# Output projection of the attention heads: seven products for eight in six of eight column pairs

## The chip, the cores and the metric

One Trainium2 chip, of which the program uses one core. The metric is the time of one execution on the device in microseconds (us). A core has five engines that run beside each other and each take their instructions in order: PE (TensorE, matrix products), DVE (VectorE), ACT (ScalarE), POOL (GpSimd) and SP (SyncE, which here only issues DMAs). DMAs move data between DRAM and the on-chip memory; matrix products write to PSUM banks, from which DVE or ACT fetch the result. "Evacuating" a bank means that fetch.

## The reference

One encoder layer over two requests of 256 tokens (512 columns here), model width 2048:

```python
xn = rmsnorm(h, norm_mix_w)
proj = xn @ w_in
y_na = neighbourhood_attention(na(0), na(1), na(2), na_rpb)      # 8 heads of 128
y_dn = gated_deltanet_bidir(...)                                  # 8 heads of 128
mixed = jnp.concatenate([y_na, y_dn.astype(h.dtype)], axis=-1) @ w_out
h = h + mixed
hn = rmsnorm(h, norm_ffn_w)
return h + (jax.nn.silu(hn @ w_gate) * (hn @ w_up)) @ w_down
```

The change concerns `mixed`, and of it the half that multiplies the attention heads `y_na` with the upper half of `w_out`. That is a product of a 2048 x 1024 matrix (transposed weights) with 1024 x 512.

## The kernel before

All activations lie transposed: features on the 128 partitions, the 512 token columns along the free side; the first 256 columns are one request, the last 256 the other. Products are made as exactly as float32 needs: each operand is split into a rounded part (`hi`) and the rest (`lo`), and `mm3` issues three matrix products for one, hi x hi, hi x lo and lo x hi. The split of a weight tile is one ACT instruction (`hi`, line 138) and one DVE subtraction (`lo`, line 139). The helper `half_gemm` makes a 128 x 512 result from a 128 x 1024 weight tile with eight times `mm3`, 24 matrix products of 512 columns:

```python
def load_w(src, shape):                                                     # 143
    raw = wp.tile([P] + shape, F32, tag="raw", bufs=3, name="w_raw")
    nc.sync.dma_start(raw, src)
    hi = wp.tile([P] + shape, F32R, tag="hi", bufs=3, name="w_hi")
    lo = wp.tile([P] + shape, F32R, tag="lo", bufs=3, name="w_lo")
    with tc.high_priority(offset=AHEAD):
        split(hi, lo, raw)
```

Each of the tags `raw`, `hi` and `lo` has three buffers, and so has the PSUM tag `g` of the pool `pg`, in which the results arise. So the fourth tile after one waits until that one's buffer is free: a weight split waits for the products of three tiles earlier, and a product waits until the result of three products earlier is evacuated. Tiles keep their engine's program order, which the scheduler fixes when the program is built; `tc.high_priority` moves instructions ahead in it. PE's order is that of the code.

Small work of other stages is spread between the products: `pump()` advances generators by one step (`chains`, `side`). While the attention half of the output projection runs, the last two heads of the recurrence (`recur`, heads 6 and 7) finish this way, and after them `finish_pair`: squares of the outputs on ACT (line 876), a reciprocal root by Newton steps on DVE (lines 880 to 882), a scaling on DVE (line 887), and after a pause of five pumps eight transposes on PE (line 90) with what follows (lines 903, 141, 142).

The stage itself, lines 950 to 972: the attention heads are read back from DRAM (`s_na`) into `nml`, split into `nmh` and `nml`, and the residual input `xT` is read into `h1`. Then, over the sixteen column tiles `i` in the order 0, 8, 1, 9, ..., one `half_gemm` each, the result is added to `h1` on DVE (line 969) and stored to DRAM as `s_h1` by a DMA on POOL (line 971):

```python
for i in pairs:                                                             # 965
    ps = pg.tile([P, T], F32, tag="g", name="ps_g")
    half_gemm(ps, w_out[i, 0], nas, True, True)
    hk = h1[i // 8][:, i % 8]
    tt(hk, hk, ps, ALU.add)
    if i not in pairs[:2]:
        nc.gpsimd.dma_start(s_h1[i], hk)
```

The next stage, lines 973 to 1031, does the other half (`half_gemm` with `dns`, the recurrence's heads), reads `s_h1` into `hk` (SP, line 1006), adds the product on DVE (line 1009), stores `s_h2` on POOL (line 1010) and prepares the operands of the feed-forward stage. That stage uses a seven-products scheme of its own (`block`), which the change does not alter.

## Time and profile before

| | |
|---|---|
| times of three runs | 2252.09, 2252.39, 2252.64 us; median 2252.39 |
| the profiled execution | 2253.6 us, of which the span from first to last instruction is 2251.8 us |
| clock of TensorE granted in it | 0.998 |
| the stage that the change rewrites | about 742 to 842 us of the span |
| the stage after it, also touched | about 842 to 932 us |
| stores of `s_h1` late in the first of them | every 5.44 us, one per `half_gemm` |

A row of the profile names line, engine, operation, `out<-in` and the shape; "x" is a count, "busy" a sum in us, "mean" in ns, and after the second bar stands the engine's idle time just before these instructions with what ended it. Matrix products overlap in the records, so the pace is read from their starts, not from their durations. A DMA row of a queue ends with the KB of one and the median us from issue to landing.

### The profile page before, as it was taken

The page shows a single profiled execution, that of the slowest core. Times are in us where ns is not written, and L with a number is a line of the kernel's source. Part 1 is how long each engine was busy: PE and PEld are TensorE (multiplying, and loading weights), DVE is VectorE, ACT ScalarE, POOL GpSimd, SP SyncE. Part 2 cuts the span into 40 slices and gives each one's busy share as a digit, 9 for nine tenths or more (in the row PEclk, how much of TensorE's full clock was granted, in tenths as well). Part 3 has the DMA queues.
Part 4 walks back from the last instruction along what each step waited for, and adds up shares of the span by engine and source line. Part 5 has one row for each costly group of instructions (what it writes and reads, how often), then busy time and mean ns, then how long its engine had stood idle before and what let it go on. Part 6 is the DMA issues. An engine that isn't in the chain of part 4 may idle for free.

```text
span 2251.8 us, 32459 instructions
## 1 busy us (share of the span) xinstructions
PE 2238.1 (99%) x12308; PEld 1918.6 (85%) x12308; DVE 1776.8 (79%) x2726; ACT 1031.3 (46%) x1550; POOL 236.6 (11%) x370
## 2 busy tenths in 40 slices
PE   9999999999999999999999999999999999999998
PEld 7888888888888888888888888888888888888888
DVE  7954799974555637888888888888888798898966
ACT  6664433333434325544444444444444464444435
POOL 1321000010000010101101111101100001001010
PEclk9999999999999999999999999999999999999999
DMA  5344322354333555677777777777777467667682
GB/s 210 130 141 144 111 97 95 100 145 133 103 104 103 195 175 190 208 205 205 200 208 200 200 192 203 216 203 204 200 197 194 147 179 210 176 179 205 176 205 86
DMA packets 112540, 381.20 MB, mean 169 GB/s; under 512 B 14048, under 2 KB 14640, under 8 KB 112128
## 3 DMA queue, kind: packets, MB, share of 16 engines
q1 hardware_dynamic: 77552, 266.25, 35.3%
q0 software_dynamic: 33680, 110.78, 23.7%
q8 instruction: 97, 1.59, 0.3%
q10 hardware_dynamic: 1152, 2.10, 0.3%
q14 instruction: 59, 0.48, 0.1%
HBM read 343.66 MB, written 35.41 MB: 168 GB/s over the span
## 4 chain that ended last, share of the span: by engine, by line
PE 91%; DVE 4%; DMA 2%; issue 1%; ACT 1%; POOL 0%; SPq 0%; DVEq 0%; ACTq 0%; POOLq 0%
PE ps_g L87 32%; PE ps_c L87 14%; PE ps_d L87 14%; PE ps_a L87 14%; PE ps_b L87 7%; PE ps_s L87 7%; DMA w_raw<-in_w_in_dram 1%; DVE w_lo L139 1%; DVE prod L587 1%; DVE W L589 1%; PE ps_o L87 1%; DMA kkq<-s_gram 1%; PE ps_s L90 1%; PE ps_e L87 0%; ACT w_hi L138 0%
## 5 line engine op out<-in xcount | busy, mean ns | idle before, releaser
L87 PE MATMUL ps_g<-xhi,w_hi 128*128 128x512 f32 x880 | 351.6, 400 | 0.0
L87 PE MATMUL ps_g<-xhi,w_lo 128*128 128x512 f32 x880 | 343.4, 390 | 0.8 <-DVE w_lo L139 0.8
L87 PE MATMUL ps_g<-xlo,w_hi 128*128 128x512 f32 x880 | 343.2, 390 | 0.6 <-DVE xlo L257 0.6
L138 ACT ACTIVATE w_hi<-w_raw 128x1024 fp32r<-128x1024 f32 x164 | 173.3, 1058 | 275.7 <-PE ps_g L87 209.6
L138 ACT ACTIVATE w_hi<-b 128x1024 fp32r<-128x1024 f32 (+1 forms) x180 | 185.8, 1032 | 237.8 <-issue 119.2
L139 DVE TENSOR_TENSOR w_lo<-w_raw,w_hi 128x1024 fp32r<-128x1024 f32 x164 | 200.4, 1222 | 111.1 <-ACT w_hi L138 110.9
L138 ACT ACTIVATE w_hi<-w_first 128x1024 fp32r<-128x1024 f32 (+1 forms) x180 | 185.4, 1030 | 180.9 <-PE ps_c L87 90.8
L139 DVE TENSOR_TENSOR w_lo<-w_first,w_hi 128x1024 fp32r<-128x1024 f32 (+1 forms) x180 | 213.8, 1188 | 60.2 <-ACT w_hi L138 56.7
L139 DVE TENSOR_TENSOR w_lo<-b,w_hi 128x1024 fp32r<-128x1024 f32 (+1 forms) x180 | 213.1, 1184 | 7.2 <-ACT w_hi L138 6.7
L87 PEld LDWEIGHTS ps_g<-xhi,w_lo 128*128 128x128 f32 x880 | 165.2, 188 | 36.8 <-DVE w_lo L139 1.3
L87 PEld LDWEIGHTS ps_g<-xhi,w_hi 128*128 128x128 f32 x880 | 165.4, 188 | 36.3 <-issue 2.9
L87 PEld LDWEIGHTS ps_g<-xlo,w_hi 128*128 128x128 f32 x880 | 165.4, 188 | 33.9 <-DVE xlo L257 1.6
L87 PE MATMUL ps_d<-xc,w_hi 128*128 128x512 f32 x704 | 175.1, 391 | 0.0
L87 PE MATMUL ps_c<-xc,w_hi 128*128 128x512 f32 x704 | 175.1, 391 | 0.0
L87 PE MATMUL ps_a<-xc,w_hi 128*128 128x512 f32 x696 | 173.1, 391 | 0.0
L87 PEld LDWEIGHTS ps_c<-xc,w_hi 128*128 128x128 f32 x704 | 129.4, 188 | 25.0
L87 PEld LDWEIGHTS ps_d<-xc,w_hi 128*128 128x128 f32 x704 | 129.3, 188 | 25.0
L87 PEld LDWEIGHTS ps_a<-xc,w_hi 128*128 128x128 f32 x696 | 127.9, 188 | 24.8
L138 ACT ACTIVATE w_hi<-w_second 128x1024 fp32r<-128x1024 f32 (+1 forms) x60 | 62.0, 1033 | 93.2 <-DVE ga L1153 50.3
L87 PE MATMUL ps_d<-xc,w_lo 128*128 128x256 f32 x704 | 98.5, 283 | 0.0
L87 PE MATMUL ps_c<-xc,w_lo 128*128 128x256 f32 x704 | 98.5, 283 | 0.0
L87 PE MATMUL ps_a<-xc,w_lo 128*128 128x256 f32 x696 | 97.4, 283 | 0.0
(390 smaller groups left out, 4209.6 us busy)
## 6 DMA issues: line engine op xcount, KB each, us to landing
w_raw<-in_w_in_dram SPq DMA_DIRECT2D x108, 512.0 KB, 3.3
b<-in_w_gate_dram SPq DMA_DIRECT2D x66, 512.0 KB, 4.1
b<-in_w_up_dram SPq DMA_DIRECT2D x66, 512.0 KB, 4.9
b<-in_w_group_dram SPq DMA_DIRECT2D x48, 448.0 KB, 4.3
w_raw<-in_w_out_dram SPq DMA_DIRECT2D x32, 512.0 KB, 3.6
w_raw<-in_w_down_dram SPq DMA_DIRECT2D x24, 512.0 KB, 3.7
w_second<-in_w_gate_dram SPq DMA_DIRECT2D x22, 512.0 KB, 7.3
w_first<-in_w_gate_dram SPq DMA_DIRECT2D x22, 512.0 KB, 4.5
```

Source lines behind the costliest of these rows:

```text
L87: pin(nc.tensor.matmul(*a, **k))
L90: pin(nc.tensor.transpose(*a))
L138: act(out=hi, in_=src, func=AF.Copy)
L139: tt(lo, src, r32(hi), ALU.subtract)
L587: stt(pv, W[:, s0:s1, s0:c], ndm[:, c:c + 1], kkq[:, c, 0, None, s0:c].broadcast_to([P, n, j]), ALU.mult, ALU.mult)
L589: nc.vector.tensor_reduce(W[:, s0:s1, c], pv, AX.X, ALU.add)
```

## The change

Column tiles are taken in pairs (j, j + 8). The first two pairs (`MIX_PLAIN = 2`) are computed as before, with the result copied out by ACT and stored without the residual. Each of the other six pairs becomes a `mix_block`: the pair's two output tiles, the two halves of the attention heads (0 to 3 and 4 to 7) and the two requests form a 2 x 2 product of blocks, and a scheme with seven products and sums of blocks is used in place of eight. Each of the seven multiplies a 128 x 512 weight tile (four heads) with 256 columns: 4 times `mm3`, 12 matrix products of 256 columns. Below they are called p0 to p6 in their order; their weights are b11, b21, `second`, `first` and its two further sums, with b22 before the last (p0 b11, p1 b21, p2 `second`, p3 `first`, p4 `first` + b22, p5 b22, p6 that sum + b21).

- Sums of token blocks (`token_sums`, once, 12 instructions on POOL, 16 for the splits) are made while the plain pairs run, from a second read of `s_na` into `nsum`.
- Sums of weight blocks: two on DVE (lines 1023, 1024), two on POOL (lines 1048, 1053). The `lo` of p5's weights (line 956) is made on POOL in place of DVE. Three sums of results are on POOL (lines 1050, 1054, 1055).
- The residual `xT` is no longer added here. The next stage reads `s_h1` on SP (line 1072) and adds `xT` by an accumulating DMA on POOL (line 964), and its buffer `hk` has three copies in place of two.

```diff
+MIX_PLAIN = 2
...
+    def w_split(src, minus=tt):
+        n = src.shape[1]
+        hi = wp.tile([P, 8, P], F32R, tag="hi", bufs=3, name="w_hi")[:, :n]
+        lo = wp.tile([P, 8, P], F32R, tag="lo", bufs=3, name="w_lo")[:, :n]
+        act(out=hi, in_=src, func=AF.Copy)
+        minus(lo, src, r32(hi), ALU.subtract)
+        return hi, lo
...
+    def token_sums(k):
+        hi, lo = (nsum[k // 2][:, k % 2, i] for i in range(2))
+        raw = r32(hi)
+        c31 = wk.tile([P, 2, L], F32, tag="cacc", name="n_s31")
+        c42 = wk.tile([P, 2, L], F32, tag="rstd", name="n_s42")
+        on_pool = nc.gpsimd.tensor_tensor
+        on_pool(c31, raw[:, :2], raw[:, 1:4:2], ALU.subtract)
+        on_pool(c42[:, 1], c31[:, 1], raw[:, 0], ALU.subtract)
+        on_pool(c42[:, 0], raw[:, 2], c42[:, 1], ALU.add)
+        split(hi[:, :2], lo[:, :2], c31)
+        split(hi[:, 2:], lo[:, 2:], c42)
...
+    def mix_out(f):
+        return na.tile([P, T], F32, tag=("qT", "kT")[f], name="mix_out")
+    def mix_block(j):
+        w4 = [w_out[i, 0][:, k:k + 4] for i in (j, j + 8) for k in (0, 4)]
+        first, second = [wk.tile([P, 4, P], F32, tag="xi", bufs=2, name=nm)
+                         for nm in ("w_first", "w_second")]
+        with tc.high_priority(offset=3 * AHEAD):
+            b11, b21, b22 = [wp.tile([P, 8, P], F32, tag="raw", bufs=3, name=nm)[:, :4]
+                             for nm in ("b11", "b21", "b22")]
+            for b, w in zip((b11, second, b21, b22), (w4[0], w4[2], w4[1], w4[3])):
+                nc.sync.dma_start(b, w)
+        with ahead():
+            tt(first, b11, second, ALU.add)
+            tt(second, second, b22, ALU.add)
+        pu = wk.tile([P, 2, L], F32, tag="rstd", name="p1_u2")
+        p34 = wk.tile([P, 2, L], F32, tag="cacc", name="p3_p4")
...
+        def times(src, x, minus=tt):
+            with ahead():
+                wh, wl = w_split(src, minus)
+            ps = pg.tile([P, T], F32, tag="g", name="ps_g")[:, :L]
+            for k, (xh, xl) in enumerate(x):
+                mm3(ps, wh[:, k], wl[:, k], xh, xl, k == 0, k == 3)
+            pump()
+            return ps
+        on_pool = nc.gpsimd.tensor_tensor
+        nc.scalar.copy(p1, times(b11, plain(0, 0)))
+        tt(o[0][:, 0], times(b21, plain(1, 0)), p1, ALU.add)
+        nc.scalar.copy(p3, times(second, summed(N_S3)))
+        nc.scalar.copy(p4, times(first, summed(N_S1)))
+        with ahead():
+            on_pool(first, first, b22, ALU.add)
+        tt(u2, times(first, summed(N_S2)), p1, ALU.add)
+        on_pool(p4, p4, u2, ALU.subtract)
+        tt(o[1][:, 0], times(b22, summed(N_S4), on_pool), p4, ALU.add)
+        with ahead():
+            on_pool(first, first, b21, ALU.add)
+        on_pool(o[1][:, 1], p4, p3, ALU.subtract)
+        on_pool(p3, p3, u2, ALU.add)
+        tt(o[0][:, 1], times(first, plain(1, L)), p3, ALU.add)
+        for f in range(2):
+            nc.gpsimd.dma_start(s_h1[j + 8 * f], o[f].rearrange("p b t -> p (b t)"))
-    for i in pairs:
+    for n, i in enumerate(pairs[:2 * MIX_PLAIN]):
         ps = pg.tile([P, T], F32, tag="g", name="ps_g")
         half_gemm(ps, w_out[i, 0], nas, True, True)
-        hk = h1[i // 8][:, i % 8]
-        tt(hk, hk, ps, ALU.add)
-        if i not in pairs[:2]:
-            nc.gpsimd.dma_start(s_h1[i], hk)
+        o = mix_out(n % 2)
+        nc.scalar.copy(o, ps)
+        nc.gpsimd.dma_start(s_h1[i], o)
+        if n < 4:
+            token_sums(n)
+    for j in range(MIX_PLAIN, 8):
+        mix_block(j)
+    def load_h1(t, i):
+        nc.sync.dma_start(t, s_h1[i])
+        plus(t, xT[i // 2][:, i % 2])
```

The scheduler decides where the new instructions stand. Three places matter. The first is POOL in the stage; before, it holds only stores of results (`s_h_101` is `s_h1`) and two sums for a later stage:

```order
L971 DMA s_h_101<-h_1_6529 128x512
L971 DMA s_h_101<-h_0_6528 128x512
L971 DMA s_h_101<-h_1_6529 128x512
L1072 DMA w_second<-in_w_gate_dram 128x1024
L1072 DMA w_first<-in_w_gate_dram 128x1024
L971 DMA s_h_101<-h_0_6528 128x512
```

Now, in the third block (`b_7214` is its b22, `b_7213` its b21, `p_p` the tile of p3 and p4, `p_u` that of p1 and u2):

```order
L1048 TENSOR_TENSOR w_first<-w_first,b_7214 128x512
L1053 TENSOR_TENSOR w_first<-w_first,b_7213 128x512
L956 TENSOR_TENSOR w_lo<-b_7214,w_hi 128x512
L1050 TENSOR_TENSOR p_p_7222<-p_p_7222,p_u_7221 128x256
L1054 TENSOR_TENSOR mix_out<-p_p_7222 128x256
L1055 TENSOR_TENSOR p_p_7222<-p_p_7222,p_u_7221 128x256
L1058 DMA s_h_101<-mix_out 128x512 x2
```

POOL has six sums and two stores in each block, in this order, and `w_lo` of p5 stands behind both sums for `first`.

The second place is ACT, where the squares of the last two recurrence heads stand (lines 876 and 877). Before:

```order
L821 ACTIVATE os<-ps_s,tab 128x128 x4
L138 ACTIVATE w_hi<-w_raw 128x1024
L828 COPY n<-ps_s 128x256 x2
L876 ACTIVATE yo,ssq<-os,rqs 128x128 x3
L138 ACTIVATE w_hi<-w_raw 128x1024
L876 ACTIVATE yo,ssq<-os,rqs 128x128 x3
```

Now, at the end of the plain pairs and in the first block (`p_u_6906` receives p0):

```order
L877 ACTIVATE yo,ssq<-os,rqs 128x128 x3
L955 ACTIVATE w_hi<-w_second 128x512
L877 ACTIVATE yo,ssq<-os,rqs 128x128
L1064 COPY mix_out<-ps_g 128x512
L955 ACTIVATE w_hi<-w_first 128x512
L877 ACTIVATE yo,ssq<-os,rqs 128x128
L1043 COPY p_u_6906<-ps_g 128x256
L877 ACTIVATE yo,ssq<-os,rqs 128x128
L955 ACTIVATE w_hi<-w_first 128x512
```

Three of the six squares have moved behind splits and copies of the first block, which wait for PE.

The third place is DVE between the first and the second block. Before, at the same work of `finish_pair` (`ev_pU` and `ev_zs` are the gates of heads 6 and 7):

```order
L139 TENSOR_TENSOR w_lo<-w_raw,w_hi 128x1024
L903 TENSOR_TENSOR yo<-ps_s,ev_pU 128x2x2x64
L903 TENSOR_TENSOR yo<-ps_s,ev_pU 128x2x128
L142 SCALAR_TENSOR_TENSOR dmix<-yo,dnw,dmix 128x512
L903 TENSOR_TENSOR yo<-ps_s,ev_zs 128x2x2x64
L903 TENSOR_TENSOR yo<-ps_s,ev_zs 128x2x128
L142 SCALAR_TENSOR_TENSOR dmix<-yo,dnw,dmix 128x512
L969 TENSOR_TENSOR h_1_6529<-h_1_6529,ps_g 128x512
```

Now (`b_7065` is b21 of the second block, `p_p_6907` belongs to the first block, line 1051 evacuates its p5 and line 1056 its p6):

```order
L956 TENSOR_TENSOR w_lo<-b_7065,w_hi 128x512
L143 SCALAR_TENSOR_TENSOR dmix<-yo,dnw,dmix 128x512
L956 TENSOR_TENSOR w_lo<-w_second,w_hi 128x512
L904 TENSOR_TENSOR yo<-ps_s,ev_zs 128x2x2x64
L904 TENSOR_TENSOR yo<-ps_s,ev_zs 128x2x128
L956 TENSOR_TENSOR w_lo<-w_first,w_hi 128x512
L1051 TENSOR_TENSOR mix_out<-ps_g,p_p_6907 128x256
L143 SCALAR_TENSOR_TENSOR dmix<-yo,dnw,dmix 128x512
L1056 TENSOR_TENSOR mix_out<-ps_g,p_p_6907 128x256
```

The evacuation of the first block's p5 (line 1051) stands behind the `w_lo` of the second block's p3 (the `w_first` row above it). In the later blocks the order is another one: the sum for `second` (line 1024), `w_lo` of b21, lines 1051 and 1056, and then `w_lo` of `second` and of `first`.

75 lines of the change are left out of this document (40 added, 35 removed).

## The prediction

> **What bounds the kernel now.** I read the page first: the busy shares and the chain that ended last.
>
> ```profile
> PE 2238.1 (99%) x12308; PEld 1918.6 (85%) x12308; DVE 1776.8 (79%) x2726; ACT 1031.3 (46%) x1550; POOL 236.6 (11%) x370
> PE 91%; DVE 4%; DMA 2%; issue 1%; ACT 1%; POOL 0%; SPq 0%; DVEq 0%; ACTq 0%; POOLq 0%
> ```
>
> PE is busy for 99% of the span and holds 91% of the chain. That is an average, so I read the two stages that the change touches next, by the windows (busy time of PE, PEld, DVE, ACT and POOL in turn, then granted clock, share of the DMA engines, GB/s).
>
> ```profile
> 742.00:842.00 100.00, 100.00 (x532) 82.91 (x531) 48.51 (x92) 27.15 (x48) 8.92 (x15) 1.00 0.55 182
> 842.00:932.00 90.00, 90.00 (x402) 74.64 (x401) 66.38 (x101) 55.23 (x88) 9.90 (x18) 1.00 0.57 186
> ```
>
> PE is the whole of both stages, DVE is half idle, ACT three quarters idle, and POOL does little but issue stores. So products taken away shorten the stage, as long as nothing new makes PE wait. I then read the pace from the timeline: two stores of `s_h1` late in the stage, and a long row of 256-column products elsewhere.
>
> ```profile
> 832.67 0.54 POOL L971 DMA_DIRECT2D s_h<-h  x1 [4.90 <-DVE h L969]
> 838.11 0.54 POOL L971 DMA_DIRECT2D s_h<-h  x1 [4.90 <-DVE h L969]
> 2198.77 12.40 PE L87 MATMUL ps_g<-aq,wd 128*128 128x256 f32 x102
> ```
>
> The stores are 5.44 us apart: one `half_gemm`, 24 products, 0.227 us each. The 102 products of 256 columns take 12.40 us, about 0.120 each once the last one's own length is taken off, and not half of 0.227.
>
> **Step 1, the products: -4.8 us.** Twelve `half_gemm`s go: 12 x 5.44 = 65.3 us. Six blocks of 84 products come: 6 x 84 x 0.120 = 60.5 us, 10.1 us a block. Seven products for eight sounds like an eighth, but the shorter products' slower pace takes back a good part. **4.8 us, 0.21% of the time, is all that the change can gain**; what follows asks what PE waits for. A measurement of this kernel can tell about 0.2%, 4.5 us, from no change.
>
> **Prices of the new instructions.** ACT's and DVE's have rows of their own shape.
>
> ```profile
> L138 ACT ACTIVATE nmh<-nml x8: 616/628/637, 737.4 to 743.4; 128x512 fp32r<-128x512 f32 x8
> L139 DVE TENSOR_TENSOR nml<-nml,nmh x8: 681/683/685, 740.1 to 744.9; 128x512 fp32r<-128x512 f32 x8
> L1057 DVE TENSOR_TENSOR u<-ps_b,p 128x256 f32<-128x256 f32 x60 | 25.5, 425 | 30.8 <-PE ps_b L87 29.5
> L1054 ACT COPY p<-ps_a 128x256 f32<-128x256 f32 x60 | 21.3, 355 | 0.9 <-PE ps_a L87 0.9
> L1134 ACT COPY p<-ps_c 128x512 f32<-128x512 f32 x60 | 34.6, 577 | 67.6 <-PE ps_c L87 65.5 <-DVE rstd L225 2.1
> L572 POOL MEMSET W<- 128x512 f32 x1 | 0.5, 526 | 0.0
> L572 POOL MEMSET W<- 128x256 f32 x1 | 0.3, 307 | 0.0
> ```
>
> A split of 512 is 0.63 on ACT and 0.68 on DVE, a sum of 512 on DVE 0.68, a sum of a bank of 256 on DVE 0.43, copies 0.36 and 0.58 on ACT. POOL adds nothing in this stage before; the nearest rows are its fills, which write 512 in 0.53 us and read nothing. A sum moves three streams. If they go together it takes 0.5 us for 512, if one after another 1.5; I take 1.0, the two reads one after the other, and 0.5 for 256, between the ends because nothing here tells more.
>
> The Trainium skill ("GPSIMD Engine Reference", Performance versus the Vector engine) has a float32 addition of 2048 at 4497 ns on GpSimd; by that an estimate for 512 is 1.12 us, and the total below would be about 1 us higher. No run shown here has such an addition.
>
> **Step 2, the stage's start: +0.3 us (0 to 1.5).** The sums of tokens need 12 POOL instructions, 4 x (1.0 + 0.5 + 0.5) = 8 us, spread over 21.8 us of plain pairs; their splits add 8 x 0.68 = 5.5 us to a DVE that is half idle. They are not needed before the third product of the first block. What can hurt stands earlier.
>
> ```profile
> 733.32 1.92 SPq L954 DMA_DIRECT2D nml<-s_na  x4
> 744.32 1.28 DVE L139 TENSOR_TENSOR nml<-nml,nmh 128x512 fp32r<-128x512 f32 x2
> 753.71 0.60 DVE L814 SCALAR_TENSOR_TENSOR r<-ps_s,tab,dvn 128x128 f32<-128x128 f32 x2
> 755.40 1.05 PE L87 MATMUL ps_s<-r,uq 128*128 128x128 f32 x8
> ```
>
> On SP a block's weight load, which waits for a buffer, now stands ahead of the heads' last reads. I count 1.5 us of delay there against 2 to 3 us of cover: the last splits of heads end at 745.6, heads being used one after another. On DVE the recurrence's `r` (753.71) stands behind a split of token sums, 0.7 us, against the 1.1 us between its end and PE's use (755.40). The 0.3 is what may come through.
>
> **Step 3, first block: +2.6 us (1.0 to 3.5).** The pair of heads that ends here passes `finish_pair`.
>
> ```profile
> 773.90 1.05 PE L87 MATMUL ps_o<-n,uq 128*128 128x128 f32 x8
> 774.55 0.87 DVE L856 TENSOR_TENSOR os<-os,ps_o 128x256 f32<-128x256 f32 x2 [3.38 <-PE ps_o L87]
> 775.06 0.40 ACT L876 ACTIVATE yo<-os,rqs 128x128 f32<-128x128 f32 x1 [3.34 <-DVE os L856]
> 775.59 0.40 ACT L876 ACTIVATE yo<-os,rqs 128x128 f32<-128x128 f32 x1
> 778.51 0.40 ACT L876 ACTIVATE yo<-os,rqs 128x128 f32<-128x128 f32 x1
> 779.03 0.17 DVE L880 TENSOR_SCALAR ssq<-ssq 128x8 f32<-128x8 f32 x1 [0.21 <-ACT yo L876]
> 781.66 1.43 DVE L887 TENSOR_TENSOR os<-os,ssq 128x256 f32<-128x256 f32 x4
> 782.99 1.04 PE L90 MATMUL ps_s<-ident,os 128*128 128x128 f32 x8
> ```
>
> Before, squares end at 778.9, scaling at 783.1, and the transposes begin as the first scaled parts arrive: nothing idles. Now five pumps are five products of 1.44 us, where they were pieces of a longer `half_gemm`. Count from the block's first product. PE ends the last `ps_o` at -1.4 (six products of 512 columns before the block). Three squares end at 0.9. The other three now stand between ACT's splits and copies: one after the split of `second` (1.5), at 2.0; one behind the copy of the last plain tile and the split of `first`, at 3.7; the last behind the copy of p0, at 4.6. Then on DVE thirteen Newton and small steps, 13 x 0.2 = 2.6, a `lo` of 0.7 and hops, to 8.25, and four scalings of 0.36, with p6's `lo` among them, to 10.3. PE reaches the transposes, in its order after p4 plus half of p5, at 7.2 + 0.7 = 7.9. They can follow the scalings one by one, so PE stops about 2.1 us, and half a split (0.45) is late after it.
>
> **Step 4, second block: +2.7 us (2.0 to 3.5).** Its p1 writes the PSUM buffer of the first block's p5, three products before. That one's evacuation (line 1051) stands on DVE behind the `lo` of the second block's p3, the `hi` of which needs the weight buffer that the second block's p0 uses. So p1 cannot start before p0 has ended and then ACT 0.63, DVE 0.68, DVE 0.43 have followed, 1.74 us, and 0.3 for the three changes of engine, of which the rows below show the shortest.
>
> ```profile
> 750.44 1.06 ACT L138 ACTIVATE w_hi<-w_raw 128x1024 fp32r<-128x1024 f32 x1 [4.99 <-PE ps_g L87]
> 751.53 1.23 DVE L139 TENSOR_TENSOR w_lo<-w_raw,w_hi 128x1024 fp32r<-128x1024 f32 x1 [0.18 <-ACT w_hi L138]
> ```
>
> ACT ends at 751.50 and DVE begins at 751.53; the hops from and to PE I take at 0.13 each. That is 2.05 us, of which the order hides nothing. After it line 1044, which evacuates p1 into `mix_out`, waits until the first block's store of that same tile has landed, 2.3 us after its issue by the row below; I put 0.3 on that, and 0.3 on the splits that it delays on DVE.
>
> ```profile
> s_h<-h POOLq DMA_DIRECT2D x14, 256.0 KB, 2.3
> hk<-s_h SPq DMA_DIRECT2D x14, 256.0 KB, 3.3
> w_second<-in_w_gate_dram POOLq DMA_DIRECT2D x22, 512.0 KB, 5.3
> ```
>
> **Step 5, blocks 3 to 6: +4.7 us (0 to 10).** One chain goes round from block to block. The `lo` of p5 on POOL is the last reader of b22's buffer; SP then loads the next block into it, 3.3 us by the reads of the same 256 KB; DVE makes `second` and behind it, in its order, `lo` of b21, lines 1051 and 1056, `lo` of `second` and of `first`: 4 x 0.68 + 2 x 0.43 = 3.6; POOL adds b22, 1.0; ACT 0.63 and DVE 0.68 split that; POOL adds b21, 1.0, and only then makes p5's `lo`, 1.0. With six hops of 0.05 that is 11.5 us a round, where PE needs 10.1. PE's lead is used up in the third block (+0.5), and three blocks pay 1.4 each. With POOL sums at 0.5 and loads at 2.3 the round is 9.0 and costs nothing; with 1.5 it is 13.0 and costs 10.
>
> **Step 6, the next stage: 0 (0 to 1).** Sixteen accumulating loads of 256 KB come in, on the POOL queue, whose nearest row is the 5.3 us for 512 KB above; the residual then arrives 3.3 + about 5 us after its issue.
>
> ```profile
> L1009 DVE TENSOR_TENSOR hk<-hk,ps_g 128x512 f32<-128x512 f32 x14 | 9.6, 685 | 8.7 <-PE ps_g L87 8.7
> ```
>
> The sums there wait for PE, never for the loads. A third buffer gives each load another 5.4 us, so the longer way is covered. Were it not, each of 14 steps could lose up to 3 us.
>
> **The sum.** -4.8 + 0.3 + 2.6 + 2.7 + 4.7 + 0 = +5.5. The profiled execution took 2253.6 us (span 2251.8), 1.2 above the median of the runs. From the median: **2257.9 us**, 2259.1 for an execution like the profiled one. With all ends together the terms reach from -1.5 to +12.7; they won't fall together, and this case's own range is 2254 to 2262.
>
> **Rivals.**
>
> *The round fits under PE.* POOL's sums go at one stream's pace, or loads land in 2.3 us: then steps 1 to 4 alone give -4.8 + 0.3 + 2.6 + 2.7 = +0.8, 2253.2 us, no change that can be told. For it: 1.0 for a POOL sum is the middle of a guess, and DVE's sums next to it cost no more than one stream each. Against it: it needs both low ends nearly whole, 9.0 to 10.1.
>
> *POOL and DVE hinder each other.* The rows above show DVE with two inputs from SBUF and POOL only issuing. If such a DVE instruction and a POOL sum cannot run side by side, a block holds 8 x 0.68 = 5.5 us of these on DVE and 3 x 1.0 + 3 x 0.5 = 4.5 on POOL: 10.0 us, in turn, in a round that already outlasts PE. I put 0.9 us a block on it, the three short POOL sums and one long one finding DVE at work half of the time; five blocks, +4.5: 2262.4 us. No row here has a POOL sum beside DVE, so nothing in this trace speaks for or against it. The Trainium skill ("SBUF — State Buffer", Who interferes with whom) states this exclusion for a DVE instruction with two SBUF inputs and a GpSimd instruction that reads SBUF; it is the rule that speaks against this change.
>
> *The other side: nothing waits.* If squares get past ACT's copies as they did before (0.53 us apart), the bank of p5 is free in time, and the round stays under 10.1 us, PE's own saving stays: 2247.6 us, faster. It decides at the first block's transposes: scaling has to be done by 7.9 us after the block's start instead of 10.3, and line 1051 has to stand ahead of the `lo`, which its order denies.
>
> *The next stage's loads come late as well*, 16 x 256 KB more through POOL's queue: 14 x 1 us on top, 2272 us or more.
>
> **How the numbers follow.** The main case has 0.42, because steps 3 and 4 follow from orders that are fixed and step 5 from sums of measured rows with one guessed price. The round under PE 0.24, hindrance 0.24, nothing waits 0.07, late loads 0.03. The range must hold the main case, most of hindrance, and the round under PE with part of steps 3 and 4 unpaid (2250): 2250 to 2266. Faster by over 4.5 us needs the full saving: 0.07. Within 4.5 us, up to 2256.9: the round under PE (0.24) and the third of the main case in which the round is short (0.14), 0.38. Slower: the rest, 0.55.
>
> **What would show it.** Step 1: 84 products in 10.1 us where nothing waits. Step 3: PE idle about 2 us before the transposes of `os`. Step 4: PE idle 2 us before p1 of the second block, released by line 1051. Step 5: stores of line 1058 about 11.5 us apart in the later blocks, and POOL sums of 512 near 1.0. Hindrance: lines 1023, 1024 and 956 on DVE, or the sums on POOL, longer when they overlap than when they don't. Step 6: line 1009 still waits for PE. The forecast is wrong if the stores come every 10.1 us, or if PE's idle time lies in other blocks than these.

## The result and the profile after

The changed kernel took 2293.0 us in the median of four runs (2291.8 to 2297.4), against 2252.5 for the kernel before: a ratio of 1.0182, 95% interval 1.0169 to 1.0194. It is 40 us slower where 5.5 were forecast, and far outside the range. The profiled execution is the longest of the four: it took 2297.4 us, its span is 2295.6, 43.8 us more than before.

The head of the page and the chain, as before:

```profile
PE 2250.4 (98%) x12524; PEld 1934.7 (84%) x12524; DVE 1805.5 (79%) x2778; ACT 1054.3 (46%) x1610; POOL 303.1 (13%) x436
PE 83%; DMA 6%; DVE 5%; issue 2%; POOL 2%; ACT 1%; SPq 0%; DVEq 0%; POOLq 0%; ACTq 0%
```

PE's share of the chain fell from 91% to 83%, and DMA's rose from 2% to 6%. The averages hide where; the windows show it. The five stretches are the plain pairs, the first block, the other five, the stage after, and the start of the feed-forward stage (busy time of PE, PEld, DVE, ACT, POOL, then granted clock).

```profile
742.80:782.80 40.00, 36.64 (x233) 29.89 (x232) 24.33 (x51) 16.83 (x39) 15.24 (x17) 0.91 0.41 119
782.80:800.10 17.30, 13.44 (x94) 13.23 (x93) 13.35 (x30) 7.49 (x20) 6.81 (x7) 0.80 0.24 76
800.10:867.60 67.50, 55.92 (x422) 52.85 (x422) 38.29 (x62) 26.14 (x51) 37.14 (x40) 0.97 0.37 119
867.60:963.40 95.80, 90.35 (x387) 72.39 (x385) 57.51 (x88) 46.78 (x75) 23.83 (x32) 0.98 0.80 224
963.40:976.00 12.60, 5.76 (x20) 4.70 (x21) 11.55 (x18) 9.86 (x17) 3.05 (x5) 0.75 0.77 244
```

PE idles in every one of them, and in three the granted clock is under 0.92. Without waits the plain part would take 33.2 us (the 99.5 of before less twelve `half_gemm`s and the transposes), the first block 11.0 with its transposes, the other five 50.4 (10.08 each), and the stage after 87.0. So the excess is 6.8, 6.2, 17.1, 8.8 us, and 9.2 more behind that, found as the time from the first feed-forward product to the end (1322.5 us against 1313.3). Less the 4.8 us that the products save, this comes to 43.3 us; PE's last product moved by 43.2.

The four longest of PE's waits (us in total, times, longest):

```profile
PE ps_a L88 <- DVE xc L140: 6.8, 1, 6.8
PE ps_s L91 <- DVE os L888: 3.9, 1, 3.9
PE ps_g L88 <- DVE mix_out L1044: 3.8, 3, 1.9
PE ps_s L88 <- DVE r L815: 3.2, 1, 3.2
```

**The plain part.** The recurrence's `r` waits; the rows are of the timeline.

```profile
754.52 1.06 POOL L999 TENSOR_TENSOR n_s<-n_s,nsum 128x256 f32<-128x256 f32 x1 [0.69 <-DVE nsum L140]
755.62 0.63 ACT L139 ACTIVATE nsum<-n_s 128x512 fp32r<-128x512 f32 x1 [3.06 <-POOL n_s L999]
756.28 2.59 DVE L140 TENSOR_TENSOR nsum<-n_s,nsum 128x512 fp32r<-128x512 f32 x2 [1.30 <-ACT nsum L139]
758.79 0.59 DVE L815 SCALAR_TENSOR_TENSOR r<-ps_s,tab,dvn 128x128 f32<-128x128 f32 x2
```

`r` stood at 753.7 us before. Now it stands behind two splits of token sums, the splits wait for ACT, and ACT waits for POOL's second set of sums. The two splits take 2.59 us where two cost 1.28 elsewhere. PE stopped for 3.6 us, and after it the granted clock stayed at half for 5.7 us, which is another 2.8.

**The first block.** PE waits for the scaling of `os`. On DVE the Newton steps stand beside POOL's sums:

```profile
788.74 1.29 POOL L1053 TENSOR_TENSOR w_first<-w_first,b 128x512 f32<-128x512 f32 x1 [1.47 <-PE ps_g L88]
788.77 1.28 DVE L168 SCALAR_TENSOR_TENSOR rs_o<-nw,rs_o 128x8 f32<-128x8 f32 x1
789.99 1.27 POOL L956 TENSOR_TENSOR w_lo<-b,w_hi 128x512 fp32r<-128x512 f32 x1
790.09 1.19 DVE L166 SCALAR_TENSOR_TENSOR nw<-rs_o,ssq 128x8 f32<-128x8 f32 x1
791.31 0.17 DVE L167 TENSOR_TENSOR nw<-nw,rs_o 128x8 f32<-128x8 f32 x1
794.02 1.94 PE L91 MATMUL ps_s<-ident,os 128*128 128x128 f32 x8 [3.86 <-DVE os L888]
```

Steps of eight columns, 0.17 us each, took 1.28 and 1.19: each ended with the POOL sum beside it. A third, line 881 at 786.3 us, took 1.00. That is the exclusion of one of the rivals, in the open. Taking every DVE instruction of the stage that lasted over 0.1 us longer than the first quartile of its form in the whole execution, and adding up what it lasted longer, gives about 10.2 us, and some 2 on POOL; the same count on the kernel before gives none.

**The other blocks.** POOL's rows by group, and a piece of the chain of waits:

```profile
L1053 POOL TENSOR_TENSOR w_first<-w_first,b 128x512 f32<-128x512 f32 x6 | 7.7, 1286 | 11.9 <-DVE w_lo L956 10.4 <-PE ps_g L88 1.5
L956 POOL TENSOR_TENSOR w_lo<-b,w_hi 128x512 fp32r<-128x512 f32 x6 | 7.7, 1280 | 0.0
...
806.10 1.30 POOL w_first L1053
807.40 1.25 POOL w_lo L956
808.67 3.02 DMA b<-in_w_out_dram
...
843.74 5.07 DMA s_h<-mix_out
```

A sum of 512 takes 1.29 us, not the 1.0 that I took. The round of step 5 is there: sum, `lo`, load of b22, and DVE's sum behind it. Beside it stands a second one, the store of `mix_out` that line 1044 waits for, 5.07 us, not 2.3.

**The stage after.** Here the chain is DMAs:

```profile
919.58 0.56 POOL hk L964
920.14 8.51 DMA s_h<-hk
928.70 2.70 DMA hk<-s_h
931.99 5.60 DMA hk<-in_xT_dram
937.71 0.70 DVE hk L1114
```

A buffer's store is issued on POOL behind the accumulating loads of the next buffers: here its sum (line 1114) ended at 918.4 us, the store was issued at 920.1, and it landed 8.5 us later (2.4 in the median before). Only then is the buffer read, added to and used again: 17.6 us from the issue of the store to the next sum. Line 1114 waits for loads now, and the feed-forward operands come 7 us late.

### The profile page after: what moved, and what is told of

The parts are those of the page before. It is cut to its first block, busy times and chain, and to the rows that moved or that the text cites. A ratio compares the mean times of both kernels' runs of the same rounds, so it can differ in the third digit from the quotient of the medians.

```text
span 2295.6 us, 33232 instructions
## 1 busy us (share of the span) xinstructions
PE 2250.4 (98%) x12524; PEld 1934.7 (84%) x12524; DVE 1805.5 (79%) x2778; ACT 1054.3 (46%) x1610; POOL 303.1 (13%) x436
## 3 DMA queue, kind: packets, MB, share of 16 engines
q0 software_dynamic: 36144, 115.50, 24.6%
## 4 chain that ended last, share of the span: by engine, by line
PE 83%; DMA 6%; DVE 5%; issue 2%; POOL 2%; ACT 1%; SPq 0%; DVEq 0%; POOLq 0%; ACTq 0%
PE ps_g L88 25%; PE ps_c L88 14%; PE ps_d L88 14%; PE ps_a L88 14%; PE ps_b L88 7%; PE ps_s L88 7%; DMA s_h<-hk 1%; DMA w_raw<-in_w_in_dram 1%; DVE prod L588 1%; DVE w_lo L140 1%; DMA hk<-in_xT_dram 1%; DVE W L590 1%; PE ps_s L91 1%; DMA kkq<-s_gram 1%; PE ps_o L88 1%
## 5 line engine op out<-in xcount | busy, mean ns | idle before, releaser
L955 ACT ACTIVATE w_hi<-b 128x1024 fp32r<-128x1024 f32 (+2 forms) x198 | 197.0, 995 | 248.6 <-issue 119.1
L955 ACT ACTIVATE w_hi<-w_first 128x1024 fp32r<-128x1024 f32 (+2 forms) x198 | 196.6, 993 | 207.9 <-PE ps_c L88 90.9
L956 DVE TENSOR_TENSOR w_lo<-w_first,w_hi 128x1024 fp32r<-128x1024 f32 (+2 forms) x198 | 227.8, 1151 | 71.8 <-ACT w_hi L955 67.1
L140 DVE TENSOR_TENSOR w_lo<-w_raw,w_hi 128x1024 fp32r<-128x1024 f32 x152 | 185.5, 1221 | 108.8 <-ACT w_hi L139 108.3
L139 ACT ACTIVATE w_hi<-w_raw 128x1024 fp32r<-128x1024 f32 x152 | 160.3, 1056 | 214.3 <-PE ps_g L88 146.5
L956 DVE TENSOR_TENSOR w_lo<-b,w_hi 128x1024 fp32r<-128x1024 f32 (+2 forms) x192 | 222.0, 1156 | 9.9 <-ACT w_hi L955 9.6
L955 ACT ACTIVATE w_hi<-w_second 128x1024 fp32r<-128x1024 f32 (+2 forms) x66 | 65.7, 995 | 102.2 <-DVE ga L1233 50.2
```

Source lines behind the costliest of these rows:

```text
L139: act(out=hi, in_=src, func=AF.Copy)
L140: tt(lo, src, r32(hi), ALU.subtract)
L955: act(out=hi, in_=src, func=AF.Copy)
L956: minus(lo, src, r32(hi), ALU.subtract)
```

## The experiments

Each kernel was timed beside the kernel before, whose medians were 2252.9 to 2253.4 us. Differences below are to these; the changed kernel stands at +40.5.

**1. The residual.** All column tiles plain, only the residual's new path kept:

```diff
-MIX_PLAIN = 2
+MIX_PLAIN = 8
...
-            nc.sync.dma_start(raw[:, i * T:i * T + T], s_na[k + 4 * i])
+            pass
...
-        if n < 4:
-            token_sums(n)
```

> All sixteen column tiles are plain half_gemms as before the change, without blocks and sums of tokens; kept are the copy of each result by ACT, its store without the residual, and the next stage's read of s_h1 with the accumulating load of xT behind it. Theory 1 (the later part of the loss, 8.8 us in the stage after and 9.2 at the start of the feed-forward stage, is a loop of its own: store of a buffer on POOL, next read into it, accumulating load, sum on DVE, store): 2268 to 2272 us, with the stage from the first product with the recurrence's heads to the first of the feed-forward stage 95 to 97 us instead of 87.0, and this stage at 99.5. Rival (that part only follows from the blocks' late stores and from POOL being late): 2252 to 2255, stage after at 87 to 88.

2265.4 us, +12.1 (ratio 1.0057, 1.0042 to 1.0072). A little under theory 1's range and far from the rival: the loop makes itself, without blocks. In the profiled execution, the longest of the four (2269.9 us), the stage after took 89.7 us, and 13.3 were lost behind it.

The other way round, the changed kernel without the accumulating load, so that its output lacks the residual:

```diff
     def load_h1(t, i):
         nc.sync.dma_start(t, s_h1[i])
-        plus(t, xT[i // 2][:, i % 2])
```

> The changed kernel without the accumulating loads: xT is added nowhere, so the output lacks the residual; s_h1 is still read back by SP and there are three buffers. Theory 1 (the accumulating load is what makes the loop longer than PE's 5.44 us a tile): 18 us less than the changed kernel, 2273 to 2277, the stage after at 87 to 88 us. Rival (the read of s_h1 behind a late store does it, with or without the addition): 2285 to 2293, the stage after still 92 us or more.

2278.3 us, +25.0: 15.5 less than the changed kernel, a little short of the 18 expected. The stage after is at 87.1 us, and what follows it takes as long as before the change (1313.5 us to PE's last product, 1313.3 before). The reads of `s_h1` alone cost nothing.

What makes the loop long? The first of these two kernels, with the store of `s_h2` on another queue:

```diff
-        nc.gpsimd.dma_start(s_h2[i], hk)
+        nc.scalar.dma_start(s_h2[i], hk)
```

> The all-plain kernel with the new residual path (2265.4 us, 12 above the kernel before), with one edit: the store of s_h2 is issued by ACT instead of POOL, so that it no longer stands behind an accumulating load that waits for its read. Theory 4 (the loop is long because of that queue): 2253 to 2257, and the stage after with its 87.0 to 88 us. Rival (the landing of the accumulating load, 5.3 us, makes the loop long by itself): 2262 to 2266.

2257.0 us (2255.1 to 2261.0), +4.0: moving the store out of POOL's queue gave back two thirds of the 12.1. In the profiled execution, the shortest of the ten, the stage after is back at 87.0 and PE waits once for 1.4 us at the start of the feed-forward stage; where the rest of the 4.0 goes in the longer ones is not shown. The accumulating loads still take 5.4 us from issue to landing (5.3 in the run before).

**2. Token sums.**

```diff
-        on_pool = nc.gpsimd.tensor_tensor
+        on_pool = tt
         on_pool(c31, raw[:, :2], raw[:, 1:4:2], ALU.subtract)
```

> The changed kernel with the twelve sums of token blocks on DVE in place of POOL. Theory 2 (the recurrence's step at 755 us waits because DVE, in its order, waits for splits of sums that POOL makes late, each sum 1.3 us and blocked by DVE's own two-input instructions): the plain part takes 33 to 35 us instead of 40.0 and the time falls by 5 to 7, to 2286 to 2288. Rival (the sums are late because the second read of s_na is late, and whoever makes them holds the recurrence up): less than 2 us gained, plain part 38 us or more.

2288.4 us, +35.1, 5.4 less; the plain part fell from 40.0 to 33.5 us. Theory 2 holds: the sums on DVE keep `r` from waiting at all.

**3. All sums on DVE**, those of the blocks and p5's `lo` too; beside the edit above:

```diff
-        on_pool = nc.gpsimd.tensor_tensor
+        on_pool = tt
         nc.scalar.copy(p1, times(b11, plain(0, 0)))
```

> The changed kernel with all arithmetic of POOL on DVE: sums of tokens, of weights and of results, and the lo of p5. Theory 3 (POOL's sums and DVE's instructions with two inputs from SBUF exclude each other, and POOL takes 1.3 us where DVE takes 0.68): the first block falls from 17.2 to 13 or less, the others from 13.5 on average to 10.5 to 11.5, the whole by 17 to 25 us to 2268 to 2276. Rival (DVE then has 10.1 us of its own work in a block and becomes the bound, or the order of buffers and evacuations holds the blocks up whoever does the sums): blocks at 12.5 us or more, the whole less than 12 us better, 2281 or more.

2275.1 us, +21.8 (runs from 2270.3 to 2283.5, the last the profiled one). Blocks of 18.0, 10.2, 10.7, 14.2, 11.1 and 10.5 us; the one of 14.2 has a stop of 2.5 us, at line 1051, and 3.4 us of half clock behind it. The other later ones came close to 10.08, which speaks for POOL as their cost. The first did not: moving the sums is no cure for it.

**4. Exclusion by itself.** The kernel before with POOL instructions that nobody waits for:

```diff
+        idle = [na.tile([P, T], F32, tag=t, name="idle") for t in ("qT", "kT")]
+        for m in range(2):
+            if i < 8:
+                nc.gpsimd.tensor_tensor(idle[m], r32(nmh[:, m]), r32(nml[:, m]), ALU.add)
+            else:
+                nc.gpsimd.memset(idle[m], 0.0)
         half_gemm(ps, w_out[i, 0], nas, True, True)
```

> The kernel before the change, with two idle POOL instructions of 512 columns ahead of each half_gemm of the stage, on buffers that nobody reads: sums of a head's two parts (two inputs from SBUF) for column tiles 0 to 7, fills for tiles 8 to 15. Theory 3 (a POOL sum and a DVE instruction with two SBUF inputs exclude each other): a lo of 128x1024 (1.22 us alone) that meets a sum takes up to 1.3 us longer, or the sum does; beside fills both keep 1.22 and 0.53; the time stays within 3 us of the kernel before, since DVE is half idle there. Rival (no exclusion, POOL is only slow): lo and sums keep 1.22 and 1.28 to 1.30 wherever they overlap.

```profile
L970 POOL TENSOR_TENSOR idle<-nmh,nml x16: 1264/1288/2288, 739.5 to 769.6; 128x512 f32<-128x512 f32 x16
L139 DVE TENSOR_TENSOR nml<-nml,nmh x6: 677/1750/1782, 739.9 to 747.8; 128x512 fp32r<-128x512 f32 x6
...
748.90 0.99 POOL L972 MEMSET idle<- 128x512 f32 x2
749.43 1.21 DVE L139 TENSOR_TENSOR w_lo<-w_raw,w_hi 128x1024 fp32r<-128x1024 f32 x1
750.57 2.14 DVE L848 SCALAR_TENSOR_TENSOR S<-S,egl,ps_s 128x128 f32<-128x128 f32 x8
```

A split of 512 with a median of 0.683 us before (681 to 685) now has one of 1.75: 1.07 longer. And the sums, 1.29 alone, reach 2.29. Beside a sum, the eight updates of line 848, which read one operand from PSUM, keep their 2.14 us (2.15 in the kernel before). The only split of weights that begins beside a fill, for 0.46 us of its length, keeps its 1.21 (1.22 alone); no split runs beside fills alone, so that fills hinder nobody rests on this one. Since nothing waits on POOL, sums and fills all ran in the first 32 us. The 32 instructions cost 4.3 us (2257.3): PE waited 2.6 us for a DVE instruction behind these splits. The expectation of 3 us was a little low, the mechanism is shown.

**5. The first block.** The transposes ten pumps later:

```diff
-        yield from pause(FIN_GAP)
+        yield from pause(FIN_GAP if h + 2 < H else 10)
```

> The changed kernel with one edit: after the scaling of the last two recurrence heads the transposes wait ten pumps instead of five, so they stand in PE's order in the second block. If the 4.1 us stall at the transposes and the slow clock behind it are what the first block loses, it falls from 17.2 to 11 to 12 us and the whole by 5 to 6 us, to 2287 to 2288. Rival (the evacuations and splits queued on DVE behind the same small steps hold the block up as well): less than 2 us gained, with other waits of PE in the first two blocks.

2294.2 us, +41.2: nothing gained, the rival. The first block fell to 14.6 us and the second rose to 15.8; evacuations stood behind the same Newton steps. Three plain pairs in place of two, so that the tail of the recurrence is over before the first block:

```diff
-MIX_PLAIN = 2
+MIX_PLAIN = 3
```

> The changed kernel with one edit: three plain pairs instead of two. Theory 6: the first block no longer has the transposes in it and falls from 17.2 to 13 or less, and one block of 13.5 us is replaced by a pair of 10.9: 6 to 8 us less in all, 2285 to 2287. Rival (the first block's loss is the start of the blocks' own round): it stays above 15, 2 to 3 us less in all, 2290.

2292.6 us, +39.6. The first block did fall, to 11.0 us, but the plain part took 57.5 where 45.1 are needed: the same transposes now stalled 2.8 us in it, with the slow clock behind, beside the token sums' stall. The time of the whole was missed by both expectations. What this leaves open is answered below.

**6. Buffers.** Two sets of `mix_out` in turn, and b22 in two buffers of its own:

```diff
-    def mix_out(f):
-        return na.tile([P, T], F32, tag=("qT", "kT")[f], name="mix_out")
+    def mix_out(f, odd=0):
+        return na.tile([P, T], F32, tag=("qT", "kT", "vT", "s1")[f + 2 * odd], name="mix_out")
...
```

> The changed kernel with two sets of mix_out in turn, so that a block's first evacuation of p1 (line 1044) no longer waits for the block before to be stored (5 us from issue to landing at 843.7 us). If that wait is a cost of its own, 3.8 us of PE's waits go: 2288 to 2290. Rival (the round through b22's buffer and POOL is as long, and takes its place): less than 1.5 us gained.

```diff
...
+            b22 = na.tile([P, 4, P], F32, tag=("vn", "s0")[j % 2], name="b22")
```

> The changed kernel with b22 in two buffers of its own instead of the shared raw ones, so that the next block's load does not wait for p5's lo on POOL. If the round of step 5 (lo on POOL, load 2.9, DVE's sums and los, POOL's sums, each 1.3) sets the pace of the later blocks, blocks 3 to 6 fall from 13.7 us on average to 12 or less and the whole by 5 to 7 us, to 2286 to 2288. Rival (in-order queues of POOL and DVE that hinder each other hold the blocks at the same pace): blocks stay above 13, less than 2 us gained.

2289.1 us, +36.1, 4.4 less; and 2284.4 us, +31.4, 9.1 less. In the first the blocks from the third on took 12.5 to 12.8, in the second 12.1 to 13.8. Both rounds were real, but neither edit brings these under 12: the expectation for b22 (12 or less) failed while its total was passed, since its plain part took 35.7 us instead of 40.0. The trace shows why: in that kernel's order on DVE, `r` (753.95 us) stands ahead of the second set's splits (756.02), and PE does not wait for it.

**7. Together.** Two versions were tried that put the parts together: no token sums on POOL, both buffers, and the residual without accumulating loads (`s_h1` filled with xT beforehand, results added to it by accumulating stores):

```diff
+    for j in range(8):
+        nc.sync.dma_start(s_h1[2 * j:2 * j + 2].rearrange("i p t -> p i t"), xT[j])
...
-        nc.gpsimd.dma_start(s_h1[i], o)
+        plus(s_h1[i], o)
...
```

> Both edits above together, sums of tokens on DVE, and the residual by accumulating stores into a prefilled s_h1; the blocks' sums stay on POOL. If the parts add up: 2293 less 4.6 (sums of tokens), 15 to 18 (residual), 5 to 10 (both edits): 2260 to 2268. Rival (the exclusion between POOL and DVE holds blocks at 13 us and more by itself): 2268 to 2274.

2266.7 us, +13.7, as the parts add up; but the four later blocks took 12.2 to 12.4 us each, with every buffer free and only the sums left on POOL. With all sums on DVE and the residual so, but the old buffers and the transposes ten pumps later:

> What the runs so far point to: all sums on DVE, the transposes ten pumps later, and the residual without an accumulating load: s_h1 is filled with xT beforehand (DRAM to DRAM) and the results are added to it by accumulating stores, so that the next stage reads a finished sum as before the change. From the run with all sums on DVE (2275.1) this takes off 13 to 18 us for the residual and 6 to 7 for the first block: 2250 to 2256, the same as the kernel before or a little under it; 2248 if no wait is left in the blocks. Rival (the accumulating stores land late, 5 us and more, and hold mix_out): blocks of 12 us, 2262 or more.

2263.1 us, +10.1, over the expected range. The stage after was at 87.4, so the accumulating stores work; the second block, with the transposes, took 17.0, and the later ones up to 12.5, at p1, which waits for line 1051.

**8. Nothing waits.** No arithmetic on POOL, `first` and `second` made by accumulating loads, both buffers, three plain pairs:

```diff
-            tt(first, b11, second, ALU.add)
-            tt(second, second, b22, ALU.add)
+        first, second = weight_sums((w4[0], w4[1], w4[2], w4[3]), lambda nm: wk.tile(
+            [P, 4, P], F32, tag="xi", bufs=2, name="w_" + nm))
...
```

> No arithmetic on POOL at all: sums of tokens, results and splits on DVE, first and second made by accumulating loads (1.4 us less on DVE a block), b22 and mix_out with buffers of their own, the residual by accumulating stores into a prefilled s_h1, and three plain pairs instead of two, so that the recurrence ends before the first block. Five blocks can gain 4.0 us of products at most. If DVE's share (9.1 of 10.1 us a block) leaves room: 2249 to 2252, a little under the kernel before. Rival (DVE's queue in its fixed order still makes PE wait 1 to 2 us a block): 2254 to 2260, slower than the kernel before by 1 to 8.

2277.6 us, +24.6, which neither theory had. Only one wait is left, four times:

```profile
PE ps_g L88 <- ACT w_hi L955: 15.9, 4, 4.2
```

The loads for `first` found its buffer taken until the last split of the block before. Each pause of some 4.3 us cost 7 us (blocks of 17.1), by the slow clock after it. With two sets of those buffers:

```diff
-            wk.tile([P, 4, P], F32, tag="xi", bufs=2, name="w_" + nm)
+            wk.tile([P, 4, P], F32, tag="xi", bufs=2, name="w_" + nm) if j % 2 else
+            na.tile([P, 4, P], F32, tag={"first": "pU", "second": "pT"}[nm], name="w_" + nm)
```

> The last kernel (no arithmetic on POOL, accumulating loads for first and second, three plain pairs) with one edit: first and second have two sets of buffers in turn, so that the accumulating loads of a block no longer wait for the last split of the block before, which made PE wait 4 times 4.3 us with a slow clock behind each. If waits and the clock behind them are all that is left: five blocks of 10.1 us, the stage at 95.5 to 97 us, the whole 3 to 4 us under the kernel before, 2249 to 2250. Rival (DVE's share or the accumulating loads still make PE wait 1 us a block): 2253 to 2256.

**2249.7 us, -3.2 (ratio 0.9986, 0.9977 to 0.9994): faster than both kernels, than the one before by a seventh of a per cent.** PE does not idle in its five blocks:

```profile
787.10:837.60 50.50, 50.50 (x422) 50.48 (x421) 42.03 (x78) 26.90 (x51) 14.86 (x17) 1.00 0.91 204
```

Five blocks in 50.5 us, 10.1 each: the products' saving is there, and it is as small as step 1 said.

**9. What POOL's sums cost alone.** That kernel with the blocks' sums back on POOL:

```diff
-        on_pool = tt
+        on_pool = nc.gpsimd.tensor_tensor
         nc.scalar.copy(p1, times(b11, plain(0, 0)))
```

> The same kernel with the blocks' five sums and the lo of p5 back on POOL, all else as in it; five blocks. Theory 3 (POOL takes 1.3 us for a sum of 512 and shuts out DVE's two-input instructions for as long, and the sums stand on the way to PE): blocks of 11.5 to 12.3 us, 7 to 11 us above the kernel without POOL sums, 2257 to 2261. Rival (with buffers free and residual and recurrence out of the way POOL's sums are hidden): within 2 us of it.

2267.1 us, +14.2, over the theory's range, for another reason: in three blocks POOL's sums stood behind an accumulating load in its queue, and PE waited up to 4.2 us for p5's `lo`. So twice more, without accumulating loads in the blocks, all on DVE:

```diff
-        first, second = weight_sums((w4[0], w4[1], w4[2], w4[3]), lambda nm: (
...
+            tt(first, b11, second, ALU.add)
+            tt(second, second, b22, ALU.add)
```

> The kernel that beat the one before (2249.7, five blocks without a wait), with first and second made by DVE's sums again instead of accumulating loads: all arithmetic on DVE, 10.5 us of DVE work in a block of 10.1. If DVE is then the bound: blocks of 10.4 to 10.8 us, 2 to 4 us above that kernel, 2251 to 2254. Rival (the order makes it worse than its load): blocks of 11.5 and more, 2257 and up.

and with five sums and the `lo` on POOL by the edit above, the only difference:

> The same with the blocks' five sums and p5's lo on POOL, and with no accumulating load in POOL's queue ahead of them, which is what spoiled the run with POOL sums before (its last two blocks, without loads in the queue, took 11.1 and 11.4 us). Theory 3 (POOL's sums, 1.3 us each and shutting out DVE, cost by themselves, with every buffer free): blocks of 11.1 to 11.6 us, 5 to 8 us above the kernel with no POOL sums, 2255 to 2258. Rival (it was the queue alone): blocks of 10.1 to 10.3, 2250 to 2251.

2252.9 us (+0.1; ratio 0.9998, 0.9988 to 1.0008) and 2262.3 (+9.4). The five blocks take 53.4 and 62.0 us:

```profile
787.60:841.10 53.50, 51.53 (x422) 50.66 (x422) 45.76 (x86) 27.83 (x51) 7.79 (x9) 1.00 0.63 138
790.40:852.30 61.90, 53.85 (x421) 51.10 (x420) 38.16 (x57) 26.36 (x51) 39.96 (x38) 1.00 0.53 120
```

Both expectations were on the right side, the second too low. POOL's sums cost 8.6 us in five blocks, 1.7 a block, where DVE has less to do and every buffer is free. In the timeline of the kernel with POOL sums:

```profile
814.45 1.07 POOL L1057 TENSOR_TENSOR mix_out<-p_p 128x256 f32<-128x256 f32 x1
814.84 1.23 DVE L956 TENSOR_TENSOR w_lo<-b,w_hi 128x512 fp32r<-128x512 f32 x1
815.99 1.22 DVE L1027 TENSOR_TENSOR w_second<-w_second,b 128x512 f32<-128x512 f32 x1
819.76 1.78 POOL L1051 TENSOR_TENSOR w_first<-w_first,b 128x512 f32<-128x512 f32 x1
820.05 0.42 DVE L1047 TENSOR_TENSOR mix_out<-ps_g,p_u 128x256 f32<-128x256 f32 x1 [0.38 <-issue]
```

A DVE instruction with two inputs from SBUF and a POOL sum beside it make each other longer (alone they take 0.69 us, and 0.74 for the sum of 256 columns); line 1047, which reads one operand from PSUM, keeps its 0.42 in the midst of a sum.

**10. The first block without POOL.** The fastest kernel with two plain pairs:

```diff
-MIX_PLAIN = 3
+MIX_PLAIN = 2
...
-            wk.tile([P, 4, P], F32, tag="xi", bufs=2, name="w_" + nm) if j % 2 else
+            wk.tile([P, 4, P], F32, tag="xi", bufs=2, name="w_" + nm) if j % 2 == MIX_PLAIN % 2 else
```

> The kernel without POOL sums and with two sets of buffers, with two plain pairs instead of three, so that the recurrence's last squares, Newton steps, scalings and transposes fall into the first block again. Theory 6 (that tail, in order on ACT and DVE with a block's splits, is what the first block loses, with POOL or without): the first two blocks lose 5 to 9 us, the whole 4 to 9 above the same kernel with three plain pairs. Rival (without POOL sums DVE has room for it): 0.8 us less than with three, by the products of one more block.

2268.8 us, +15.9, 19 above the same kernel with three, far more than expected. Its first block took 16.5 us, with 3.8 at the transposes, and no sum ran on POOL:

```profile
PE ps_s L91 <- DVE os L888: 3.8, 1, 3.8
```

That is theory 6, for the first block. The second took 23.5, with a wait of 11.0 for weights; I put that down, without having tested it, to the buffers `pU` and `pT` that I gave to `first` and `second`, which the recurrence still uses then, so it says nothing on the theory and spoils the total. The last four blocks took 10.08 each.

## Why the prediction was wrong, step by step

The steps that failed are 6, 5 and 2, in the order of what they missed: the next stage was put at 0 and lost 18.0 us, the later blocks at 4.7 and lost 14.3, the start at 0.3 and lost 6.8.

*Step 1, the products, -4.8.* Right. 84 products take 10.08 us wherever nothing waits, and the kernel with five blocks keeps 3.2 of the 4.0 that its products save.

*Step 2, the stage's start, +0.3.* It was 6.8. The place was named, `r` behind a split of token sums, but it was priced as 0.7 us of work. The split is an instruction that waits: for ACT, which waits for POOL, whose sums begin only when the second read of the heads has landed (748.9 us) and then take 3.0 us a set. The step failed in asking how long the split takes and not when it can begin. The clock then added 2.8.

*Step 3, the first block, +2.6.* It was 6.2. The wait at the transposes is there and the reason too. I counted 2.1 us; it was 3.9, since PE came 7.3 us after the block's start (7.9 counted) and the scalings ended at 11.7 (10.3 counted). Three small DVE steps lasted until POOL's sums beside them ended, together 3.0 us longer than alone, but this does not make POOL the cause of the wait: without a sum on POOL it was 3.8 in the last experiment, where DVE's own sums stood between the Newton steps. What I left out is the clock after it, about 2.3 us.

*Step 4, the second block, +2.7.* It lost 2.8, but not as told. Its p1 lost 1.1, released by the copy of p0 on ACT, and began at 802.58 us, before line 1051 had run:

```profile
802.17 0.35 ACT L1043 COPY p_u<-ps_g 128x256 f32<-128x256 f32 x1
802.58 0.50 PE L88 MATMUL ps_g<-nm,w_hi 128*128 128x256 f32 x2 [0.92 <-ACT p_u L1043]
802.91 0.42 DVE L1051 TENSOR_TENSOR mix_out<-ps_g,p_p 128x256 f32<-128x256 f32 x1
```

Another 1.5 went after p6, where the third block's p0 waited for line 1049. The wait for line 1051 came at p1 of the fourth block, 1.7 us. The sum of this step is right by luck.

*Step 5, blocks three to six, +4.7 (0 to 10).* They lost 14.3. The round was right, and buffers of its own for b22 took 5.2 us off the six blocks (the rest of the 9.1 lies outside them, most of it in the plain part). Two of its terms were short: sums of 1.29 instead of 1.0, and DVE's share 3.6, which grows when sums run beside it. A second round, through the store of `mix_out`, I priced at 0.6 in all; two sets of that buffer gave back 4.4.

*Hindrance, the rival at 0.24.* It was no rival but a part of everything: about 10.2 us of longer DVE instructions, not all of them on PE's path. I asked only for its price in a full block (0.9); measured with every buffer free, POOL's sums cost 1.7 us a block, by their length and the exclusion together. The rule of the Trainium skill ("SBUF — State Buffer", Who interferes with whom) told it ahead, down to the one operand from PSUM that escapes; the traces agree, 0.68 to 1.75 us in experiment 4. It should have been weighed as a fact to price, not as a way it could go. The other figure that I quoted from the Trainium skill ("GPSIMD Engine Reference", Performance versus the Vector engine) would have served better as well: the estimate of 1.12 us for a sum of 512 falls short of the measured 1.29, but less than my 1.0.

*Step 6, the stage after, 0 (0 to 1).* It lost 18.0, the largest miss; the rival that the loads come late priced it at 14, but had a chance of 0.03. Every size in it was about right (3.3 for the read, 5.5 for the accumulating load). What failed is the sentence that the sums wait for PE, never for the loads: that was read from a trace in which nothing came behind the read, and in which the store of a buffer stood alone in POOL's queue. I added the load's length to the read's and compared it with a buffer's time; I did not walk round the loop store, read, addition, sum, store, with the queue in which two of these stand. The store's move to another queue gave back 8.1 of 12.1 us.

Together: the forecast held two rounds and three orders, each with its cover, and was short in most of them because each was costed with the others at rest. None of the terms held the slower clock behind a stop. Nor were the ends added up rightly: the steps' ranges together reach from -1.8 to +14.7, not from -1.5 to +12.7; the result lies beyond either.

## What to carry to other kernels

A scheme that makes seven products of eight can save a fifth of a per cent of the whole here, and single waits that it brings cost more: count the saving first, and put work only on engines and into buffers that have a full step to spare. Walk round each loop of buffers with everything that stands ahead in its queues; a DMA issued on an engine that works in order carries the wait of the one before it. An instruction in an order is costed by when its inputs are there, not by its length. DVE work that took an operand from PSUM kept its length beside POOL's sums in these traces: that is the work to put beside them.

## What the hardware showed that I had not expected

**The clock after a pause.** PE's pace nearly halves after a long enough stop. In the changed kernel, 256-column products before and after the transposes' stall:

```profile
789.29 0.40 PE L88 MATMUL ps_g<-nsum,w_hi 128*128 128x256 f32 x2
789.53 0.28 PE L88 MATMUL ps_g<-nsum,w_lo 128*128 128x256 f32 x1
789.65 0.40 PE L88 MATMUL ps_g<-nsum,w_hi 128*128 128x256 f32 x2
...
796.83 0.41 PE L88 MATMUL ps_g<-nsum,w_lo 128*128 128x256 f32 x1
797.04 0.63 PE L88 MATMUL ps_g<-nsum,w_hi 128*128 128x256 f32 x2
797.47 0.41 PE L88 MATMUL ps_g<-nsum,w_lo 128*128 128x256 f32 x1
```

Three products start in 0.36 us before, in 0.64 after, until about 799 us. In this kernel, stops of 2.2, 3.1, 3.6, 4.1 and 7.2 us, from one product's start to the next one's, were followed by 3.4 to 5.7 us of it, shorter ones by none. A stop of 4 us so costs about 6.5.

Length alone does not decide. In the kernel with three plain pairs a stop of 2.9 us was followed by none; in the one with token sums on DVE a stop of 1.6 was. The granted clock is halved in whole steps of 3.41 us, and all of a trace's steps lie on one grid. Two steps of that grid in the changed kernel, and what came after the second:

```profile
826.28:829.70 3.42, 1.75 (x15) 1.57 (x14) 2.80 (x6) 1.41 (x3) 1.56 (x3) 1.00 0.17 61
846.77:850.18 3.41, 1.44 (x10) 1.06 (x9) 1.02 (x2) 0.46 (x2) 0.14 (x1) 1.00 0.07 28
850.18:853.59 3.41, 3.41 (x16) 3.33 (x17) 1.55 (x2) 1.50 (x3) 2.37 (x2) 0.50 0.27 78
```

PE idles 1.67 us of the first, and the clock stays; it idles 1.97 of the second, and the clock is halved in the next. Between 600 and 1100 us of all the traces here, each of the 45 steps at full clock in which PE idled 1.69 us or more was followed by half clock, and none in which it idled 1.68 or less. Elsewhere this count by gaps does not always hold: in the first kernel of experiment 9 a step with 1.80 us idle, at 1869 us, kept the clock, and at the ends of the executions, where products of one column stand, 0.85 us was enough. In the stretch of the change, then, half a step of idling was enough, and a stop of 2 or 3 us was free when the grid cut it in two. The Trainium skill ("TensorE: Matmul & The Clock Gate", Part 1) has the rule, half rate after an idle window of about 3.4 us; the traces agree with the window's length, but PE need not be idle for all of it.

**Accumulating DMAs into DRAM** landed in 6.2 us for 256 KB in the median of the fastest kernel, and hid wholly, where the accumulating loads of the same size into SBUF in experiment 1 took 5.3 and did not.
